# Reading relative-bias tables straight from one reversed row per head in DRAM

## The chip, the core and the metric

The kernel runs on one core of a Trainium2 chip. The core has five engines that work side by side, each through its own list of instructions in order: TensorE (PE in the profile, matrix products; its weight loads are listed as PEld), VectorE (DVE), ScalarE (ACT), GpSimd (POOL) and SyncE (SP). In this kernel every DMA is handed over by SyncE, so SyncE's list is also the order in which transfers are started; 16 DMA engines then move the data. The metric is the time of one execution on the device in microseconds (us).

## What is computed

One layer of a hybrid decoder on 512 tokens of 1024 features, in float32: a normalisation modulated by a conditioning vector, one input projection, two attention branches, a gated merge with an output projection, a squared-ReLU MLP, and a last normalisation. The change touches the additive bias of the two attention branches. Each of the 16 heads has a bias that depends on the distance between query and key alone, by a bucket of that distance:

```python
bias = rel_bias[t5_bucket(dist)][..., :SWA_Q_HEADS]            # sliding window, 8 heads
s = jnp.where(mask, s + bias, -jnp.inf)                        # window of 128 keys
...
table_b = rel_bias[:, SWA_Q_HEADS:].T                          # block attention, 8 heads
bias_own = table_b[:, t5_bucket(dist_own)]
s_own = jnp.where(dist_own >= 0, s_own + bias_own, -jnp.inf)
```

So along a diagonal of the score matrix the bias is the same: row p of a 128-row block of queries has the same list of numbers as row p + 1, moved by one key.

## The kernel before

**The list per head.** The host gives a one-hot table `onehot` of 33 rows by 1024 columns: 640 columns hold the bucket of each distance for the block attention, 384 those for the sliding window, and the 33rd row the mask. At the start of the kernel TensorE multiplies it with the bias table (L358), which gives `prv`, 16 heads by 512 columns, twice. ScalarE copies it to `rv` in SBUF (L359), and SyncE stores both halves to `rvd` in DRAM (L360): 16 rows of 1024 numbers, one row per head.

**The spread.** From there two DMAs inside DRAM make 128 copies of each row: `tsd` (L394, 8 heads x 128 x 384 numbers, for the sliding-window heads) and `tmd` (L427, 8 heads x 128 x 640 numbers, for the others). Their access pattern has the heads outermost, then the 128 copies with step 0, then the columns.

**The load per head.** `toeplitz` (L430 to L434) fills one tile of 128 partitions by 256 columns (`ts`) or 512 columns (`tm`) per head by a DMA whose row step is one number shorter than a row of the copies, so partition p reads its copy moved by p. The tiles have two buffers: a load waits until the head before the last has used its bias.

**The use.** For each head and each of its four blocks of 128 queries TensorE makes the scores (L449, `sa` or `sb`), and one VectorE instruction adds the bias and takes the row maximum (L450). A sliding-window head has blocks of 128, 256, 256 and 256 keys, a head of the block attention 128, 256, 384 and 512; a narrower block takes the last columns of the tile. ScalarE then takes the exponential (L454), TensorE transposes (L479) and multiplies with the values (L490).

**The work around it.** Every float32 product is made as three products of a high and a low part (L76 to L78); ScalarE and VectorE split each operand into the parts (L71, L72). The first stage loads the conditioning weights (`ad`, L268), makes the normalised input `hT` and the query projection of the sliding window (`g0p`). Then come the keys and values of the sliding window: `kvr` is loaded (L397), split into two pairs of weights `kvw0` and `kvw1`, and multiplied to `pkv`; `vaf` (L410) is ScalarE's copy of the values, which TensorE turns (`pva`, L416). The queries are split and their lower half is copied across partitions by a DMA (`qa`, L225), the keys likewise (`ka`, L234). The function `run` (L612) then goes through the 16 heads and between the parts of a head advances a list of dense work, in this order: values of the block attention (`proj_v`, loads `vbr`, products `pv`), its queries and keys (`proj_qk`, loads `qkr` at L550, weights `qkw`, products `pqk`), the gates (`gated`, loads `gr`), and so on. Weight loads of 1 MB (`kvr`, `vbr`, `qkr`, `gr` and the last of the `ad` tiles) share three buffers in turn (`raw`), and the split weights of 1024 columns two pairs (`wide`).

**What sets the order.** In the first stage the order on TensorE and SyncE is the written one (L331 to L391). After that a planner orders each engine's list when the program is built, from a simulated time line and the order in the code; L394 comes after the first stage, L427 inside `proj_v`. The order is fixed then, and at run time an engine waits at the first instruction of its list that isn't ready.

Of the kernel before, what the change touches and what calls it, by code (L numbers as in the profile page):

```python
# [10 lines left out]
F32 = mybir.dt.float32  # L11
F32R = mybir.dt.float32r
AF = mybir.ActivationFunctionType
ALU = mybir.AluOpType

P = 128
# [5 lines left out]
SCALE = HD ** -0.5  # L22
NH = 8
# [7 lines left out]
W_MOBA = 640  # L31
W_SWA = 384
# [5 lines left out]
def decoder_layer(ctx: ExitStack, tc: tile.TileContext, x, c, ada_w, ada_b, norm1_g, norm2_g, w_in,  # L38
# [3 lines left out]
    V, A, G, SY = nc.vector, nc.scalar, nc.gpsimd, nc.sync  # L42
# [3 lines left out]
    dr = ctx.enter_context(tc.tile_pool(name="dr", bufs=1, space=bass.MemoryType.DRAM))  # L46
# [3 lines left out]
    def bank(name):  # L50
        return ps.tile([P, 512], F32, tag="bank", name=name)

    def raw(name):
        return p0.tile([P, 2048], F32, tag="raw", name=name, bufs=3)
# [5 lines left out]
    def wide(name):  # L60
        return ptile(p0, [P, KT, P], name, "w", 2)

    def small(name):
        return ptile(p0, [P, 512], name, "s", 2)

    def scratch(name, dt=F32):
        return p0.tile([P, 512], dt, name=name, tag="t", bufs=3)

    def split(hi, lo, src):

        A.activation(hi, src, AF.Copy)  # L71
        V.tensor_tensor(lo, src, hi.bitcast(F32), op=ALU.subtract)  # L72
# [67 lines left out]
    def rows(stack):  # L140
        pst = bank("pst2")
        nc.tensor.transpose(pst[:, :64], stack, ident[:64, :64])
        V.tensor_copy(cols, pst[:, :64])
# [66 lines left out]
    with ExitStack() as sa:  # L210
# [26 lines left out]
        va = pa.tile([P, NT, 4, HD], F32R, name="va")  # L237
        sink = pz.tile([P, NH], F32, name="sink")
        rvd = dr.tile([16, W_MOBA + W_SWA], F32, name="rvd")
        tmd = dr.tile([NH, P, W_MOBA], F32, name="tmd")  # L240
        tsd = dr.tile([NH, P, W_SWA], F32, name="tsd")

        with ExitStack() as ss:
            pq = ss.enter_context(tc.tile_pool(name="pq", bufs=1))
# [110 lines left out]
            for s in range(2):  # L355
                cc = slice(s * 512, (s + 1) * 512)
                prv, rv = bank(f"prv{s}"), scratch(f"rv{s}")
                nc.tensor.matmul(prv[:16], rbx, oh[:, cc], start=True, stop=True)  # L358
                A.activation(rv[:16], prv[:16], AF.Copy)  # L359
                SY.dma_start(rvd[:, cc], rv[:16])  # L360
            rows(stack)
            next(cols_[0])
            px = bank("px0")
# [14 lines left out]
            for f in range(KT):  # L378
                for i, _ in enumerate(project(f, 2 if f == 0 else 0, NT)):
# [4 lines left out]
                    if i == 2 and f + 2 in starts:  # L384
                        n = starts[f + 2]
# [3 lines left out]
                if f + 2 < KT:  # L389
                    wgt[f + 2] = g0_split(f + 2)  # L390
            sm.close()  # L391

            wt = W_MOBA + W_SWA
            SY.dma_start(tsd, bass.AP(tensor=rvd.tensor, offset=rvd.offset + W_MOBA,  # L394
                                      ap=[[wt, NH], [0, P], [1, W_SWA]]))
            kvr = raw("kvr").rearrange("p (k n) -> p k n", k=KT)
            SY.dma_start(kvr, w0[:, :, C_KA:C_KA + 2 * P])  # L397
            pkv = []
            for s in range(2):
                w = wide(f"kvw{s}")  # L400
# [21 lines left out]
        attnT = tuple((p0.tile([P, 4, S], F32R, name=f"at{b}h", tag=f"at{b}h"),  # L422
                       p0.tile([P, 4, S], F32R, name=f"at{b}l", tag=f"at{b}l")) for b in range(2))

        def spread_moba():
            wt = W_MOBA + W_SWA
            SY.dma_start(tmd, bass.AP(tensor=rvd.tensor, offset=rvd.offset + 8 * wt,  # L427
                                      ap=[[wt, NH], [0, P], [1, W_MOBA]]))

        def toeplitz(src, h, w, n, name):  # L430
            t = pt_.tile([P, n], F32, name=f"{name}{h}", tag="tz", bufs=2)
            SY.dma_start(t, bass.AP(tensor=src.tensor, offset=src.offset + h * P * w + P - 1,
                                    ap=[[w - 1, P], [1, n]]))
            return t  # L434

        class Head:
            def __init__(self, name, q, k, g, v, dst, j, blocks, groups, widths, bias, sk):
                self.__dict__.update(locals())
                self.rows = slice(g * 64, g * 64 + 64)
                self.p = pt_.tile([P, 1280], F32, name="p" + name, tag="p", bufs=2)  # L440
                m = pz.tile([P, 4], F32, name="m" + name, tag="m", bufs=3)
                sums = pz.tile([P, 4], F32, name="u" + name, tag="u", bufs=3)
                neg = pz.tile([P, 4], F32, name="n" + name, tag="n", bufs=3)
                p, b = self.p, bias
                for i, (o, w) in enumerate(blocks):
                    e = (i + 1) * P
                    pb = bank(f"s{name}{i}")
                    for n in range(2):
                        nc.tensor.matmul(pb[:, :w], q[g][:, i * P:e], k[n][g][:, e - w:e], start=n == 0, stop=n == 1)  # L449
                    V.tensor_tensor_reduce(p[:, o:o + w], pb[:, :w], b[:, b.shape[1] - w:], scale=SCALE,  # L450
                                           scalar=-3e38 if sk is None else sk, op0=ALU.add, op1=ALU.max,
                                           accum_out=m[:, i:i + 1])
                    V.tensor_scalar(neg[:, i:i + 1], m[:, i:i + 1], -1.0, None, op0=ALU.mult)  # L453
                    A.activation(p[:, o:o + w], p[:, o:o + w], AF.Exp, bias=neg[:, i:i + 1],  # L454
                                 accum_out=sums[:, i:i + 1])
                if sk is not None:
                    es = pz.tile([P, 4], F32, name="e" + name, tag="es", bufs=2)
                    A.activation(es, neg, AF.Exp, bias=sk)
                    V.tensor_add(sums, sums, es)
                V.reciprocal(sums, sums)  # L460
                for i, (o, w) in enumerate(blocks):
                    if i == 3:
                        A.activation(p[:, o:o + w], p[:, o:o + w], AF.Copy, scale=sums[:, i:i + 1])
                    else:
                        V.tensor_scalar(p[:, o:o + w], p[:, o:o + w], sums[:, i:i + 1], None, op0=ALU.mult)
# [34 lines left out]
        def swa_head(n):  # L500
            j, g = n // 2, n % 2
            h = g * 4 + j
            return Head(f"a{h}", qa[j], ka, g, lambda kb: va[:, kb, 2 * g:2 * g + 2].rearrange("p c d -> p (c d)"), attnT[0], j,
                        [(0, 128), (128, 256), (384, 256), (640, 256)],
                        [[(0, (0, 1)), (1, (1, 2))], [(2, (2, 3)), (3, (3,))]], (256, 256, 256, 128),
                        toeplitz(tsd, h, W_SWA, 256, "ts"), sink[:, h:h + 1])

        def moba_head(n):
            i, g = n // 2, n % 2
            q, k = qk[i]  # L510
            return Head(f"b{n}", q, k, g, lambda kb: vb[:, kb, i, 2 * g:2 * g + 2].rearrange("p c d -> p (c d)"), attnT[1], i,
                        [(0, 128), (128, 256), (384, 384), (768, 512)],
                        [[(0, (0, 1, 2, 3))], [(1, (1, 2, 3)), (3, (3,))], [(2, (2, 3))]], (512, 384, 256, 128),
                        toeplitz(tmd, n, W_MOBA, 512, "tm"), None)


        def proj_v(half):
            pv = [bank(f"pv{half}{b}") for b in range(2)]
            wr = raw(f"vbr{half}").rearrange("p (k n) -> p k n", k=KT)
            SY.dma_start(wr, w0[:, :, C_VB + half * 256:C_VB + half * 256 + 256])  # L520
            if half == 0:
                spread_moba()
            for kk in range(4):
                w = tuple(v.rearrange("p (k n) -> p k n", k=2) for v in small(f"vw{half}{kk}"))
                split(w[0], w[1], wr[:, 2 * kk:2 * kk + 2])
                for k in range(2):
                    f = 2 * kk + k
                    for t in range(NT):
                        mm3(pv[t // 2][:, t % 2 * 256:t % 2 * 256 + 256], token(hT, f, t), at(w, slice(None), k),
                            first=f == 0 and t % 2 == 0, last=f == KT - 1, skip_group_check=True)  # L530
                if kk == 3:
                    for b in range(2):
                        for t in range(2):
                            i = slice(2 * half, 2 * half + 2)
                            split(vb[:, 2 * b + t, i, 0::3], vb[:, 2 * b + t, i, 1:3],
                                  pv[b][:, t * 256:t * 256 + 256].rearrange("p (i g d) -> p i g d", i=2, g=2))
                yield
# [125 lines left out]
    with ExitStack() as sb:  # L663
        pb = sb.enter_context(tc.tile_pool(name="pb", bufs=1, reuse_waits="tile"))
# [141 lines left out]
    for ci, (f0, f1) in enumerate(CHUNKS):  # L806
# [15 lines left out]
        for f in fs:  # L822
            w, ph = start(f)
# [4 lines left out]
        if not last:  # L828
            for half in range(2):
                pm = [bank(f"mo{ci}{half}{t}") for t in range(NT)]  # L830
                for f in range(f0, f1):
# [4 lines left out]
                    w = small(f"mow{ci}{half}{f}")  # L836
# [5 lines left out]
        else:  # L842
            ws = []
            for b in range(2):
                w = (p0.tile([P, 2, D], F32R, name=f"ml{b}h", tag=f"at{b}h"),
                     p0.tile([P, 2, D], F32R, name=f"ml{b}l", tag=f"at{b}l"))
                wr = raw(f"ml{b}").rearrange("p (k n) -> p k n", k=2)
                SY.dma_start(wr, wm[:, f0 + 2 * b:f0 + 2 * b + 2, :])
                for k in range(2):
                    for h in range(2):  # L850
                        cc = slice(h * 512, (h + 1) * 512)
# [6 lines left out]
            for t in range(NT):  # L858
                o = [slot(4 + 2 * (t % 2) + h, f"o{t}{h}") for h in range(2)]
                cuts = ((0, 512), (512, 1024)) if t < NT - 1 else ((0, 512), (512, 768), (768, 1024))  # L860
                sq, n = ssq[:, 4 * (t % 2):4 * (t % 2) + 4], len(cuts) - 1
# [73 lines left out]
```

## Time and profile before

| | us |
|---|---|
| three runs | 755.54, 755.74, 754.61 |
| median of the runs | 755.54 |
| the profiled execution, its own time | 753.28 |
| span of its instructions | 751.5 |
| TensorE busy | 713.4 (95%) |
| VectorE busy | 458.6 (61%) |
| ScalarE busy | 346.2 (46%) |

The profile is of one execution. Its span runs from the first to the last instruction, and the rest of the execution's own time lies around it. Rows give the line of the code (L450 is line 450), the engine, and "out <- in" by the names above. An engine's idle time is put down to what ended it ("<- DMA qkr" means that a transfer into `qkr` landed last). A busy TensorE isn't one at its peak; the clock it was granted stands beside it, 1.00 for the full one. DMA share is the mean busy share of the 16 DMA engines.

### The profile page before, as it was taken

To read this page: it belongs to the slowest core of one execution; us is meant where nothing else is said; L and a number is where in the kernel's file an instruction comes from. 1 tells how busy PE (TensorE), PEld (TensorE's weight loads), DVE (VectorE), ACT (ScalarE), POOL (GpSimd) and SP (SyncE) were. 2 spreads that over 40 slices of the span, in tenths; PEclk is the share of its full clock that TensorE was granted. 3 is DMA by queue.
4 is the path that set the end of the run, shared out by engine and by line. 5 is a ranking of instruction groups with operands and counts; after the bars stand their busy time and mean duration, and the time that the engine had idled before them with its cause. 6 is when DMAs were issued, how large, how long until landed. Compare 5 with 4: busy or idle time off the path is not lost.

```text
span 751.5 us, 9331 instructions
## 1 busy us (share of the span) xinstructions
PE 713.4 (95%) x3458; PEld 597.7 (80%) x3458; DVE 458.6 (61%) x957; ACT 346.2 (46%) x641; POOL 28.3 (4%) x40
## 2 busy tenths in 40 slices
PE   3789799999999999999999999999999999999996
PEld 1568788987788788888889888888888888888885
DVE  4862688788586975874468584253562627425765
ACT  4542687765777772343255443222342314222424
POOL 2220000000000000000030000000000000000001
PEclk9999899999899999999999999999999999999999
DMA  8986633374444575443513461333313233315103
GB/s 305 305 258 248 191 92 93 96 226 147 140 127 126 171 276 198 154 155 112 168 56 94 133 223 56 113 113 112 108 62 111 63 112 106 113 57 167 57 1 112
DMA packets 93210, 104.40 MB, mean 139 GB/s; under 512 B 3043, under 2 KB 71723, under 8 KB 93164
## 3 DMA queue, kind: packets, MB, share of 16 engines
q1 hardware_dynamic: 93164, 103.80, 44.2%
q8 instruction: 27, 0.44, 0.3%
q14 instruction: 19, 0.16, 0.1%
HBM read 98.22 MB, written 6.36 MB: 139 GB/s over the span
## 4 chain that ended last, share of the span: by engine, by line
PE 79%; DMA 8%; ACT 4%; SPq 3%; DVE 3%; issue 1%; POOLq 0%; POOL 0%; ACTq 0%; DVEq 0%
PE ph L77 8%; PE ph L78 8%; PE ph L76 8%; PE mo L78 7%; PE mo L77 7%; PE mo L76 7%; PE pg L76 3%; PE pg L78 3%; PE pg L77 3%; DMA qkr<-in_w_in_dram 2%; SPq L268 2%; DMA ad<-in_ada_w_dram 2%; PE py L78 2%; PE py L76 2%; PE py L77 2%; PE pqk L76 2%
## 5 line engine op out<-in xcount | busy, mean ns | idle before, releaser
L811 ACT ACTIVATE r<-ph 128x512 f32<-128x512 f32 x32 | 18.8, 586 | 41.2 <-PE ph L78 26.8
L814 DVE TENSOR_TENSOR r<-r 128x512 f32<-128x512 f32 x32 | 21.9, 688 | 18.2 <-ACT a2h L813 8.0
L156 DVE SCALAR_TENSOR_TENSOR ac<-a,cs,ac 128x256 f32<-128x256 f32 x56 | 26.8, 478 | 2.4 <-ACT ac L154 1.8
L296 DVE SCALAR_TENSOR_TENSOR pac<-ad,cs,pac 128x256 f32<-128x256 f32 (+1 forms) x42 | 21.4, 522 | 9.1 <-ACT pac L294 8.7
L722 DVE TENSOR_TENSOR rs<-mo,g2row 128x512 f32<-128x512 f32 x24 | 15.9, 684 | 8.8 <-PE mo L78 8.8
L186 DVE SCALAR_TENSOR_TENSOR ma<-mw,cs,ma 128x512 f32<-128x512 f32 x28 | 21.0, 749 | 0.5
L126 POOL TENSOR_TENSOR rstd<-rstd,mhalf 128x1 f32<-128x1 f32 x12 | 7.0, 587 | 375.2 <-DVE rstd L125 375.2
L454 ACT ACTIVATE pb<-pb,nb 128x128 f32<-128x128 f32 (+3 forms) x32 | 17.8, 557 | 7.2 <-DVE nb L453 6.8
L76 PE MATMUL g0p<-hTh,g0h 128*128 128x512 f32 (+1 forms) x36 | 15.1, 421 | 3.0 <-ACT hTh L71 3.0
L454 ACT ACTIVATE pa<-pa,na 128x256 f32<-128x256 f32 (+1 forms) x32 | 15.3, 478 | 3.2 <-DVE na L453 3.0
L723 DVE TENSOR_TENSOR x_sb<-x_sb,rs 128x512 f32<-128x512 f32 x24 | 16.1, 681 | 0.0
L450 DVE CUSTOM_DVE_ANT_0 pb<-sb,tm 128x128 f32<-128x128 f32 (+3 forms) x32 | 15.0, 486 | 0.2 <-PE sb L449 0.2
L450 DVE CUSTOM_DVE_ANT_0 pa<-sa,ts,sink 128x256 f32<-128x256 f32 (+1 forms) x32 | 13.6, 444 | 1.9 <-PE sa L449 1.8
L77 PE MATMUL g0p<-hTl,g0h 128*128 128x512 f32 (+1 forms) x36 | 14.1, 392 | 0.1
L78 PE MATMUL g0p<-hTh,g0l 128*128 128x512 f32 (+1 forms) x36 | 13.8, 384 | 0.0
L449 PE MATMUL sb<-qk,qk 128*128 128x128 f32 (+3 forms) x64 | 12.9, 331 | 0.0
L449 PE MATMUL sa<-ka,qa 128*128 128x256 f32 (+1 forms) x64 | 11.7, 297 | 0.0
L301 PEld LDWEIGHTS pac<-ones_r,acc 128*128 128x128 f32 x32 | 5.0, 224 | 8.3 <-DVE acc L296 5.7
L284 POOL TENSOR_TENSOR g0l<-g0r,g0h 128x512 fp32r<-128x512 f32 x8 | 10.3, 1293 | 27.6 <-ACT g0h L283 27.6
L301 PE MATMUL pac<-ones_r,acc 128*128 128x1 f32 x32 | 5.3, 274 | 6.1 <-DVE acc L296 6.1
L852 DVE TENSOR_TENSOR ml<-ml,g2row 128x512 f32<-128x512 f32 x8 | 5.1, 687 | 9.9 <-DMA ml<-in_w_mlp_out_dram 9.9
L723 POOL TENSOR_TENSOR x_sb<-x_sb,rs 128x512 f32<-128x512 f32 x4 | 5.0, 1290 | 157.0 <-DVE rs L722 157.0
(1599 smaller groups left out, 2431.7 us busy)
## 6 DMA issues: line engine op xcount, KB each, us to landing
mi<-in_w_mlp_in_dram SPq DMA_DIRECT2D x16, 1024.0 KB, 5.6
mo<-in_w_mlp_out_dram SPq DMA_DIRECT2D x14, 1024.0 KB, 5.1
ad<-in_ada_w_dram SPq DMA_DIRECT2D x16, 512.0 KB, 7.3
a<-in_ada_w_dram SPq DMA_DIRECT2D x16, 512.0 KB, 5.2
gr<-in_w_in_dram SPq DMA_DIRECT2D x8, 1024.0 KB, 6.3
mw<-in_ada_w_dram SPq DMA_DIRECT2D x8, 1024.0 KB, 5.2
x_sb<-in_x_dram SPq DMA_DIRECT2D x8, 512.0 KB, 6.6
qkr<-in_w_in_dram SPq DMA_DIRECT2D x4, 1024.0 KB
```

The lines of the kernel that those rows point to most:

```text
L76: nc.tensor.matmul(o, w[0], m[0], start=first, stop=False, **kw)
L77: nc.tensor.matmul(o, w[0], m[1], start=False, stop=False, **kw)
L78: nc.tensor.matmul(o, w[1], m[0], start=False, stop=last, **kw)
L156: V.scalar_tensor_tensor(acc, ad[:, k], cs[:, k:k + 1], acc, op0=ALU.mult, op1=ALU.add)
L186: V.scalar_tensor_tensor(acc, t[:, k], c1, acc, op0=ALU.mult, op1=ALU.add)
L296: V.scalar_tensor_tensor(part_ if k < KT - 1 else acc, ad(k), cs[:, k:k + 1], part_, op0=ALU.mult, op1=ALU.add)
L449: nc.tensor.matmul(pb[:, :w], q[g][:, i * P:e], k[n][g][:, e - w:e], start=n == 0, stop=n == 1)
L450: V.tensor_tensor_reduce(p[:, o:o + w], pb[:, :w], b[:, b.shape[1] - w:], scale=SCALE, scalar=-3e38 if sk is None else sk, op0=ALU.add, op ...
L454: A.activation(p[:, o:o + w], p[:, o:o + w], AF.Exp, bias=neg[:, i:i + 1], accum_out=sums[:, i:i + 1])
L723: add.tensor_tensor(x_sb[:, t, cc], x_sb[:, t, cc], tm, op=ALU.add)
L811: A.activation(r, ph, AF.Relu)
L814: V.tensor_mul(r, r, r)
```

## The change

The copies `tsd` and `tmd` and the DMAs that fill them are gone. `rv` is now made by VectorE, and with its columns in reverse; the two halves are stored in each other's place, so each row of `rvd` as a whole runs backward. The load of a head reads 128 rows straight from the one row of that head, each beginning one number after the row before, so the rows overlap. With the list reversed this step forward has the effect of the old step backward; the columns of the tile then stand in reverse, and the VectorE instruction reads its bias operand backward.

```diff
-        tmd = dr.tile([NH, P, W_MOBA], F32, name="tmd")
-        tsd = dr.tile([NH, P, W_SWA], F32, name="tsd")
...
-                A.activation(rv[:16], prv[:16], AF.Copy)
-                SY.dma_start(rvd[:, cc], rv[:16])
+                V.tensor_copy(rv[:16], prv[:16, ::-1])
+                SY.dma_start(rvd[:, 512 - s * 512:1024 - s * 512], rv[:16])
...
-            wt = W_MOBA + W_SWA
-            SY.dma_start(tsd, bass.AP(tensor=rvd.tensor, offset=rvd.offset + W_MOBA,
-                                      ap=[[wt, NH], [0, P], [1, W_SWA]]))
...
-        def spread_moba():
-            wt = W_MOBA + W_SWA
-            SY.dma_start(tmd, bass.AP(tensor=rvd.tensor, offset=rvd.offset + 8 * wt,
-                                      ap=[[wt, NH], [0, P], [1, W_MOBA]]))
-
-        def toeplitz(src, h, w, n, name):
+        def toeplitz(h, c0, n, name):
+
             t = pt_.tile([P, n], F32, name=f"{name}{h}", tag="tz", bufs=2)
-            SY.dma_start(t, bass.AP(tensor=src.tensor, offset=src.offset + h * P * w + P - 1,
-                                    ap=[[w - 1, P], [1, n]]))
+            SY.dma_start(t, bass.AP(tensor=rvd.tensor, offset=rvd.offset + h * (W_MOBA + W_SWA) + c0,
+                                    ap=[[1, P], [1, n]]))
             return t
...
-                    V.tensor_tensor_reduce(p[:, o:o + w], pb[:, :w], b[:, b.shape[1] - w:], scale=SCALE,
+                    V.tensor_tensor_reduce(p[:, o:o + w], pb[:, :w], b[:, w - 1::-1] if w < b.shape[1] else b[:, ::-1], scale=SCALE,
                                            scalar=-3e38 if sk is None else sk, op0=ALU.add, op1=ALU.max,
...
-                        toeplitz(tsd, h, W_SWA, 256, "ts"), sink[:, h:h + 1])
+                        toeplitz(h, 1, 256, "ts"), sink[:, h:h + 1])
...
-                        toeplitz(tmd, n, W_MOBA, 512, "tm"), None)
+                        toeplitz(NH + n, 1 + W_SWA, 512, "tm"), None)
...
-            if half == 0:
-                spread_moba()
```

## The prediction

> **What bounds the kernel now.** I read the page first, then the waits of TensorE, the chain, and the timelines around the place they name.
>
> ```profile
> PE 713.4 (95%) x3458; PEld 597.7 (80%) x3458; DVE 458.6 (61%) x957; ACT 346.2 (46%) x641; POOL 28.3 (4%) x40
> PE pva L416 <- ACT vaf L410: 5.0, 1, 5.0
> PE pkv L76 <- ACT kvw0h L71: 2.7, 1, 2.7
> ```
>
> TensorE is busy 95% of the span, so only its few gaps can pay. The last two lines are the longest of its waits between 35 and 110 us: 5.0 us for the tile vaf and, earlier, 2.7 us for kvw0h. The chain says what ended last before the longer one:
>
> ```profile
> 44.30 10.09 DMA vbr<-in_w_in_dram
> ...
> 64.76 17.15 DMA qkr<-in_w_in_dram
> 82.00 1.06 ACT qkw01h L71
> 83.08 0.61 ACT vaf L410
> 83.73 1.12 PE pva L416 x4
> ```
>
> vaf needs nothing from qkr. It stands behind qkw01h in ScalarE's order, and qkw01h waits for a 1 MB weight load that the chain dates 17.15 us back. The timelines of SyncE, ScalarE, TensorE and VectorE (start, duration, what, wait before):
>
> ```profile
> 44.30 0.52 SPq L520 DMA_DIRECT2D vbr<-in_w_in_dram  x1
> 44.92 3.11 SPq L394 DMA_DIRECT2D tsd<-rvd  x1
> 48.13 6.49 SPq L427 DMA_DIRECT2D tmd<-rvd  x1
> 54.71 16.29 SPq L550 DMA_DIRECT2D qkr<-in_w_in_dram  x2
> 71.09 3.47 SPq L225 DMA_DIRECT2D qa<-qa0l  x1
> 77.82 1.06 ACT L71 ACTIVATE qkw00h<-qkr 128x1024 fp32r<-128x1024 f32 x1 [7.14 <-DMA qkr<-in_w_in_dram]
> 69.66 0.39 PE L78 MATMUL pkv<-hTh,kvw0l 128*128 128x512 f32 x1
> 74.65 0.39 PE L78 MATMUL pkv<-hTh,kvw1l 128*128 128x512 f32 x1
> 78.47 0.28 PE L78 MATMUL pv<-vw01h,hTl 128*128 128x256 f32 x1
> 83.73 1.12 PE L416 MATMUL pva<-ident,vaf 128*128 128x128 f32 x4 [4.98 <-ACT vaf L410]
> 45.48 0.47 DVE L296 SCALAR_TENSOR_TENSOR acc<-ad,cs,pac 128x256 f32<-128x256 f32 x1
> 58.52 1.21 DVE L72 TENSOR_TENSOR kvw1l<-kvr,kvw1h 128x1024 fp32r<-128x1024 f32 x1
> ```
>
> Between vbr and qkr stand the two spread copies, tsd and tmd. SyncE hands vbr over in 0.52 us but is held 3.11 and 6.49 us by the spreads, and 16.29 us by the two qkr loads behind them. I read this as a queue that is full, so that everything later (qa0l at 71.09) waits too. What the queue does in that time is in the table by stretches (length, busy us of PE, PEld, DVE, ACT, POOL, granted clock, DMA share, GB/s; the sum is that of six stretches from 85 to 280); the last line is from the list of DMA issues, with KB and us to landing:
>
> ```profile
> 54.00:65.00 11.00, 8.04 (x36) 6.66 (x35) 4.56 (x5) 4.79 (x7) 1.35 (x1) 0.84 0.53 204
> 57.00:62.00 5.00, 4.70 (x21) 4.17 (x22) 3.27 (x3) 2.21 (x4) 0.51 (x1) 0.66 0.53 205
> 79.00:84.00 5.00, 0.27 (x2) 0.27 (x2) 3.43 (x4) 2.45 (x4) 0.00 (x0) 0.85 0.46 125
> 84.00:89.00 5.00, 5.00 (x24) 4.86 (x24) 4.88 (x14) 4.82 (x8) 0.00 (x0) 0.50 0.32 67
> 85.00:145.00 60.00, 60.00 (x397) 55.18 (x396) 48.66 (x168) 46.89 (x121) 1.63 (x3) 0.96 0.40 113
> 240.00:260.00 20.00, 18.41 (x96) 15.38 (x95) 17.81 (x49) 17.97 (x36) 0.00 (x0) 1.00 0.46 132
> sum 195.00, PE 189.60 PEld 164.32 DVE 153.36 ACT 144.57 POOL 4.23; mean PE 31.60 PEld 27.39 DVE 25.56 ACT 24.09 POOL 0.71
> gr<-in_w_in_dram SPq DMA_DIRECT2D x8, 1024.0 KB, 6.3
> ```
>
> For 11 us half of the DMA engines move 204 GB/s and the rest stand idle. By the shapes in the code the spreads write 8 x 128 x (384 + 640) numbers of 4 bytes, 4.19 MB, which at 204 GB/s is 20.6 us. The stretch from 84 to 89 shows a second price: after the 5 us gap TensorE runs at 0.50 of its clock.
>
> *The skill on this.* The Trainium skill (DMA: Bandwidth & Descriptors, Rules for kernel authors) says that a DMA whose outermost dimension is under 16 is confined to that many engines; here it is 8 heads, and the share of 0.53 agrees with that. Spread over all engines at twice the rate, 4.19 MB would take 10 us, both qkr loads would be there before 78.5, and taking the spreads away would save nothing; the row of 204 GB/s is what gives the change its worth.
>
> **The change, part by part.**
>
> *The two spreads go* (L394, L427). qkr's first load then follows vbr on SyncE. Its buffer, the third of the raw ones, was last read by the sum acc that ended at 45.95, so it can be issued at about 46; behind vbr, which landed at 54.4 (44.30 + 10.09), it lands by 54.4 + 6.3 (the 1 MB row) = 60.7 at the latest. The second load takes kvr's buffer, free when kvw1l ends at 59.73, and lands by 66.0. ScalarE's splits of them then wait for weight buffers only (two in the pair): qkw00h from 70.05 (last matmul on kvw0l), qkw01h from 75.04 (on kvw1l), so vaf ends at 75.04 + 1.06 + 0.61 = 76.7, before TensorE has done pv at 78.75. The copies of qa and ka that the first scores need, held behind qkr on SyncE until 71.09, go out as soon as their splits end. So the 4.98 us go. What is late next is TensorE's own work. With the gap goes the half clock: 0.27 us before 84, 5.00 us up to 89 at 0.50, and a little after: 5.3 / 2 = 2.7 us. **Sum of this part: 4.98 + 2.7 = 7.7 us.** From 85 to 145 TensorE is busy without a break, and the later loads are issued as buffers come free, so I let all later work move with it.
>
> *The first gap (2.7 us) stays.* It ends with vbr, queued ahead of the spreads, so their packets come behind it. By 0, at the least; bounded above by the whole gap and its half clock (rival A).
>
> *The copy of the rows moves from ScalarE to VectorE, reversed* (L359), and each half is stored in the other's place; two issues as before.
>
> ```profile
> 4.32 3.57 PE L358 MATMUL prv<-oh,rbx 33*16 33x512 f32 x4 [1.58 <-DMA oh<-in_onehot_dram]
> 9.03 1.05 ACT L359 ACTIVATE rv<-prv 16x512 f32<-16x512 f32 x2
> 9.13 3.13 DVE L296 SCALAR_TENSOR_TENSOR pac<-ad,cs,pac 128x512 f32<-128x512 f32 x4 [5.97 <-ACT pac L294]
> 31.71 8.46 DMA ad<-in_ada_w_dram
> ```
>
> VectorE stands idle 5.97 us, and prv is complete at 7.9 in it, so at least the first copy and most of the second fit in. A backward read from PSUM isn't in the trace: between 0.5 us each (ScalarE's) and twice that. Were they put behind the first sums instead, VectorE would be 1 to 2 us late at 9 to 13; what covers that is the stream of ad loads, which the chain follows up to 40.17 (31.71 + 8.46), and without it the 1 to 2 us would count. I take 0.
>
> *The bias loads read overlapping rows.* Their count, shape and issue stay; 128 pieces of 1 or 2 KB now come from 1.5 to 2.6 KB of DRAM.
>
> ```profile
> tm<-tmd SPq DMA_DIRECT2D x8, 256.0 KB, 2.7
> g1row<-in_ada_b_dram SPq DMA_DIRECT2D x2, 256.0 KB, 5.9
> 97.58 0.33 SPq L432 DMA_DIRECT2D ts<-tsd  x1
> 105.31 0.32 SPq L432 DMA_DIRECT2D ts<-tsd  x1
> ```
>
> Reading one row 128 times is in the trace: g1row, a row of 2 KB sent to all partitions, takes 5.9 us, tm now 2.7. Two buffers give a load about one head's time, 105.31 − 97.58 = 7.7 us. So 0; a load would have to take over 7.7 us, beyond the upper row, to be late. The first load now waits on SyncE for the store of rvd, as tsd did at 44.92, and for its memory, which the first stage had; what is queued behind it then is rival B.
>
> *VectorE reads the bias backward* (L450), 64 times.
>
> ```profile
> L450 DVE CUSTOM_DVE_ANT_0 pb<-sb,tm 128x512 f32<-128x512 f32 x8 | 5.5, 684 | 0.0
> L450 DVE CUSTOM_DVE_ANT_0 pb<-sb,tm 128x384 f32<-128x384 f32 x8 | 4.4, 549 | 0.2 <-PE sb L449 0.2
> ```
>
> A column costs (684 − 549) / 128 = 1.05 ns, one element after the other; nothing in that speaks for a price on direction. Lower bound 0. Upper: every column twice, 8 x 896 + 8 x 1280 = 17,408 columns (the blocks of the heads in the code), 18.3 us of VectorE. It is busy 81% from 85 to 145, so that hides there, but at 240 to 260 (17.81 of 20) some 2 us would show. I take 0, nearest to the forward rows.
>
> **Sum:** 753.3 (the profiled execution's own time, span 751.5) − 7.7 = 745.6. The median of the runs is 755.5, 2.2 above that execution; on their scale I forecast 755.5 − 7.7 = **747.8**, own range 745 to 750.
>
> **The rivals.**
>
> *A. The early gap goes as well.* A new planned order may let ScalarE split kvr before vbr; DRAM writes also no longer run beside the loads. Against: vbr's packets were queued before the spreads. Price: 2.7 us, and the loss of clock behind it, (1 − 0.66) x 5 us in 57 to 62, 1.7 us. Time 747.8 − 4.4 = 743.4.
>
> *B. A wait on SyncE takes the spreads' place.* In the order of the code the first bias load comes before the qkr loads. Planned so, it holds SyncE until its memory is free, at the latest when the first stage's last product is done (second row below: g0p).
>
> ```profile
> 84.50 1.63 PE L449 MATMUL sa<-ka,qa 128*128 128x128 f32 x6
> 67.85 0.39 PE L78 MATMUL g0p<-hTh,g0l 128*128 128x512 f32 x1
> ```
>
> That is 68.24, and qkr's first load lands at 68.24 + 6.3 = 74.5. Now the first scores start 84.50 − 77.82 = 6.7 us after qkw00h; from 74.5 that makes 81.2, a gap of 2.5 us after 78.75, with half clock behind it, 1.7 us as after the first gap. Of the 7.7 us 4.2 are given back: 755.5 − 3.5 = 752.0. For it: the code's order; against: the planner already put qkr ahead. By the Trainium skill (TensorE: Matmul & The Clock Gate, What's actually happening) the clock drops after an idle window of about 3.4 us; by that, the gap alone would count, 750.3. The trace differs: 2.7 us of idling before 57 were followed by a mean of 0.66 in 57 to 62.
>
> *C. Nothing gained:* the 5 us turn up again at a later wait (VectorE has 2.2 us left in 240 to 260). For it speaks that a delay shared by all engines can let one of them catch up; against, that TensorE had no break from 85 to 145. 755.5.
>
> *D. Slower: the backward read costs several times a forward one.* It would decide once VectorE has no room in the heads' stretch, 85 to 280, where it is busy 153.4 of 195 us: 41.6 us, plus the 7.7 gained, at 18.3 us per further column time, so from 3.7 times on. At four times: 54.9 − 41.6 − 7.7 = 5.6 us lost, 761. Against: the 1.05 ns.
>
> **How the numbers follow.** Forecast 0.52, A 0.15, B 0.13, C 0.11, D and other ways to lose 0.09. Range: A less the runs' spread of 1.1 us (754.61 to 755.74) gives 742.3, B plus it 753.1; outside lie C and D, 0.20. A measurement of this kernel tells about 0.2%, 1.5 us, from no change: forecast, A and B are faster (0.80), C the same (0.11), D slower (0.09).
>
> **What would show it.** In the changed profile: no DMA at half share after vbr; 4.19 MB less written to HBM; each qkr issue under 1 us unless a buffer isn't free; no 5 us wait of pva for vaf, and no clock of 0.50 after it; L450 still at 684 ns for 512 columns; tm landing in 3 to 6 us. The forecast is wrong if TensorE still has a gap of some us between the last pv of the first half and the first scores, or if its waits after 145 grow by what was saved.

## The result and the profile after

| | before | after |
|---|---|---|
| median of four runs (us) | 755.08 | 746.21 |
| lowest and highest (us) | 751.73, 755.74 | 745.23, 747.35 |
| the profiled execution, its own time (us) | 753.28 | 745.23 |
| span (us) | 751.5 | 743.5 |

The ratio is 0.9892, with a 95% interval from 0.9859 to 0.9925. The unchanged pair was timed twice more on other chips, beside the experiments below: 0.9921 (0.9899 to 0.9943) and 0.9935 (0.9908 to 0.9962). The three medians lie 8.9, 6.3 and 5.9 us below those of before; by the ratios it is 8.2, 6.0 and 4.9. The forecast was 7.7, and the intervals of the two repeats end at 7.6 and 6.9 us, a little short of it. Four executions in the groups of this document took 1029 to 4053 us; the medians count them, the ratios do not.

The page of the changed kernel; after it stand its waits of TensorE between 35 and 110 us (what TensorE waited for: us in total, times, longest):

```profile
PE 709.7 (95%) x3458; PEld 595.6 (80%) x3458; DVE 459.1 (62%) x959; ACT 344.6 (46%) x639; POOL 28.7 (4%) x40
HBM read 94.03 MB, written 2.16 MB: 129 GB/s over the span
```

The same line of the page of before:

```profile
HBM read 98.22 MB, written 6.36 MB: 139 GB/s over the span
```

And the waits:

```profile
PE pac L299 <- DVE acc L294: 1.5, 1, 1.5
PE ta L470 <- DVE pa L456: 1.2, 1, 1.2
PE pkv L76 <- ACT kvw0h L71: 1.0, 1, 1.0
PE pkv L76 <- ACT kvw1h L71: 0.2, 1, 0.2
```

Of the 6.36 MB written before, 4.20 MB are gone: the two spread copies. Of the waits, the 5.0 us of `pva` for `vaf` is gone altogether. The wait for `kvw0h` is still there, shorter in this execution. A new one has come, 1.2 us of the first transposes (`ta`) for VectorE.

The timelines of SyncE and ScalarE around the place (start, duration, what, idle time before with its releaser):

```profile
44.36 0.57 SPq L511 DMA_DIRECT2D vbr<-in_w_in_dram  x1
47.24 12.48 SPq L539 DMA_DIRECT2D qkr<-in_w_in_dram  x2
65.31 0.52 SPq L225 DMA_DIRECT2D qa<-qa0l  x1
65.92 1.02 SPq L423 DMA_DIRECT2D ts<-rvd  x2
```

```profile
67.83 1.06 ACT L71 ACTIVATE qkw00h<-qkr 128x1024 fp32r<-128x1024 f32 x1 [1.31 <-PE pkv L77]
72.82 1.06 ACT L71 ACTIVATE qkw01h<-qkr 128x1024 fp32r<-128x1024 f32 x1 [1.33 <-PE pkv L77]
73.90 0.60 ACT L405 ACTIVATE vaf<-pkv 128x512 f32<-128x512 f32 x1
```

`qkr` now goes out at 47.24 where before it was 54.71. The 12.48 us are its second load, which waits for the buffer of `kvr`; nothing else is held. The splits of `qkr` are released by TensorE ("<-PE pkv"), that is by weight buffers coming free, and no longer by the DMA. So `vaf` ends at 73.90 + 0.60 = 74.50, and TensorE reaches its transposes later than that. First the tile's row of after, then that of before (count, ns of one as min/median/max, from first start to last):

```profile
L411 PE MATMUL pva<-ident,vaf x4: 272/272/273, 76.7 to 77.0; 128*128 128x128 f32 x4
```

```profile
L416 PE MATMUL pva<-ident,vaf x4: 421/421/477, 83.7 to 84.4; 128*128 128x128 f32 x4
```

The same four transposes start 7.0 us earlier, and take 272 ns where they took 421, because no half clock follows a gap any more. The stretches of after (length, busy us of PE, PEld, DVE, ACT, POOL, granted clock, DMA share, GB/s):

```profile
54.00:65.00 11.00, 9.74 (x50) 7.73 (x49) 4.96 (x6) 5.39 (x8) 1.34 (x1) 1.00 0.45 141
57.00:62.00 5.00, 4.79 (x29) 3.94 (x28) 2.93 (x3) 1.81 (x3) 0.11 (x1) 1.00 0.23 57
74.00:84.00 10.00, 10.00 (x86) 10.00 (x85) 9.46 (x30) 8.21 (x18) 0.52 (x1) 1.00 0.51 134
84.00:89.00 5.00, 3.76 (x22) 3.02 (x21) 3.96 (x14) 4.98 (x19) 0.00 (x0) 1.00 0.64 157
```

From 74 to 84 TensorE is busy without a break at full clock; that is the stretch in which it stood still for 5 us. Between 57 and 62 the DMA engines have little to do, because both `qkr` loads are either done or still waiting for their buffer.

How the 8.0 us between the two spans come about: 7.0 us are there when `pva` starts. About 2.7 us are added by the half clock that before showed from 84 to 89 (5.3 us busy at 0.50, counted as in the prediction) and after shows no more. The new wait of `ta` takes 1.2 us back. That is 8.5, and the rest of the span changes little: from 250 us to the end TensorE's products start 8.1 us earlier than before (median over the products of each stretch of 10 us).

The 7.0 us are more than the wait of 4.98 because TensorE was 2.0 us ahead before it came to that wait: the early gap for `kvw0h` was smaller in this execution, 1.0 us, with no loss of clock behind it. This early gap is not the same in every execution, as the experiments show, so it is not put down to the change.

### The profile page after: what moved, and what is told of

The parts are those of the page before. It is cut to its first block, busy times and chain, and to the rows that moved or that the text cites. A ratio compares the mean times of both kernels' runs of the same rounds, so it can differ in the third digit from the quotient of the medians.

```text
span 743.5 us, 9326 instructions
## 1 busy us (share of the span) xinstructions
PE 709.7 (95%) x3458; PEld 595.6 (80%) x3458; DVE 459.1 (62%) x959; ACT 344.6 (46%) x639; POOL 28.7 (4%) x40
## 4 chain that ended last, share of the span: by engine, by line
PE 84%; ACT 4%; DMA 4%; DVE 3%; SPq 2%; issue 1%; POOL 0%; POOLq 0%; ACTq 0%; DVEq 0%
PE ph L77 8%; PE ph L76 8%; PE ph L78 8%; PE mo L78 7%; PE mo L76 7%; PE mo L77 7%; PE pg L76 3%; PE pg L78 3%; PE pg L77 3%; PE pqk L76 2%; PE py L78 2%; PE pqk L77 2%; PE py L76 2%; PE pqk L78 2%; PE py L77 2%
## 5 line engine op out<-in xcount | busy, mean ns | idle before, releaser
L76 PEld LDWEIGHTS g0p<-hTh,g0h 128*128 128x128 f32 x36 | 8.0, 222 | 5.1 <-ACT hTh L71 4.5
L470 PE MATMUL tb<-ident,pb 128*128 128x128 f32 x80 | 10.6, 274 | 0.3 <-DVE mb L441 0.3
```

What stands on the lines that cost most here:

```text
L76: nc.tensor.matmul(o, w[0], m[0], start=first, stop=False, **kw)
```

## The experiments

Each median stands beside runs of the kernel before on the same chip. Runs with spreads "read by nobody" do extra work whose result is not used.

**The theory** is the prediction's: the spreads run on half of the DMA engines, hold SyncE and delay the `qkr` loads, and TensorE waits for these. **Its rivals:** the bytes cost time wherever they are moved; the planner's new order brought the gain; the new form of the loads or of the copy brought or cost something.

### The spreads kept, but on all engines

The 128 copies become the outermost dimension. Bytes, destinations and the order of every engine stay as before.

```diff
-            SY.dma_start(tsd, bass.AP(tensor=rvd.tensor, offset=rvd.offset + W_MOBA,
-                                      ap=[[wt, NH], [0, P], [1, W_SWA]]))
+            SY.dma_start(tsd.rearrange("h p w -> p h w"), bass.AP(tensor=rvd.tensor, offset=rvd.offset + W_MOBA,
+                                                                  ap=[[0, P], [wt, NH], [1, W_SWA]]))
...
-            SY.dma_start(tmd, bass.AP(tensor=rvd.tensor, offset=rvd.offset + 8 * wt,
-                                      ap=[[wt, NH], [0, P], [1, W_MOBA]]))
+            SY.dma_start(tmd.rearrange("h p w -> p h w"), bass.AP(tensor=rvd.tensor, offset=rvd.offset + 8 * wt,
+                                                                  ap=[[0, P], [wt, NH], [1, W_MOBA]]))
```

> The kernel before with one thing changed: the two spreads write the same 4.19 MB with the 128 copies outermost instead of the 8 heads. The order of every engine's list is that of before. Queue theory (the spreads hold the queue because they run on half of the DMA engines): DMA share near 1 after vbr, the spreads done by about 64 us, both qkr loads landed by about 72, no 5 us wait of TensorE for vaf and no half clock after it; 755.1 - 7.7 = 747.4, between 746 and 749. Planner theory (the gain came from the new order of the lists): 755, since the order is the old one. Traffic theory (the gain is that of 4.19 MB less to move): 755, since the bytes are the same.

Measured: 749.67 beside 753.78, ratio 0.9946 (0.9923 to 0.9968). Its waits, its timelines of SyncE and ScalarE, its stretches, and its list of DMA issues (KB, us from issue to landing):

```profile
PE pva L416 <- ACT vaf L410: 2.6, 1, 2.6
```

```profile
47.23 3.29 SPq L427 DMA_DIRECT2D tmd<-rvd  x1
50.61 12.42 SPq L550 DMA_DIRECT2D qkr<-in_w_in_dram  x2
...
77.05 1.06 ACT L71 ACTIVATE qkw01h<-qkr 128x1024 fp32r<-128x1024 f32 x1 [2.67 <-DMA qkr<-in_w_in_dram]
78.13 0.60 ACT L410 ACTIVATE vaf<-pkv 128x512 f32<-128x512 f32 x1
```

```profile
54.00:57.00 3.00, 1.33 (x6) 0.48 (x4) 2.29 (x3) 3.00 (x5) 1.34 (x1) 1.00 1.07 146
57.00:62.00 5.00, 5.00 (x30) 4.50 (x31) 2.27 (x3) 1.15 (x2) 0.00 (x0) 1.00 1.00 338
```

```profile
tmd<-rvd SPq DMA_DIRECT2D x1, 2560.0 KB, 22.5
```

What follows: with the order of all instructions and all the bytes unchanged, 4.1 us are gained. The changed kernel gained 6.3 in the same comparison (753.78 to 747.52), so some two thirds of the gain hang on the engines the spreads ran on (the two intervals overlap; the wait that is left, 2.6 us, is what tells the two apart). Neither the planner nor the bytes can have brought that part. The 749.67 lies outside the 746 to 749 that the queue theory gave: it had the second `qkr` load there by 72, and `qkw01h` waited for it until 77.05.

The other third is left, and the trace shows that the spreads did not take half the time on twice the engines. All engines are busy (1.07 and 1.00), but in one stretch they move only 146 GB/s. The large spread landed at 47.23 + 22.5 = 69.7, `qkw01h` still waits for a DMA, and `vaf` ends at 78.7, 4 us later than in the changed kernel.

The rule that the prediction cited (the Trainium skill, DMA: Bandwidth & Descriptors, Rules for kernel authors: an outermost dimension under 16 confines the DMA to that many engines) agrees with the share, 0.53 before and 1.00 here. What the prediction worked out from it, that on all engines the spreads would cost nothing, does not hold.

### The spreads with the heads as 4 x 2

The heads were to be split into two dimensions, 4 and 2, so that only four engines would be used.

```diff
-            SY.dma_start(tsd, bass.AP(tensor=rvd.tensor, offset=rvd.offset + W_MOBA,
-                                      ap=[[wt, NH], [0, P], [1, W_SWA]]))
+            SY.dma_start(tsd.rearrange("(a b) p w -> a b p w", b=2), bass.AP(tensor=rvd.tensor, offset=rvd.offset + W_MOBA,
+                                      ap=[[2 * wt, 4], [wt, 2], [0, P], [1, W_SWA]]))
...
-            SY.dma_start(tmd, bass.AP(tensor=rvd.tensor, offset=rvd.offset + 8 * wt,
-                                      ap=[[wt, NH], [0, P], [1, W_MOBA]]))
+            SY.dma_start(tmd.rearrange("(a b) p w -> a b p w", b=2), bass.AP(tensor=rvd.tensor, offset=rvd.offset + 8 * wt,
+                                      ap=[[2 * wt, 4], [wt, 2], [0, P], [1, W_MOBA]]))
```

> The kernel before with the heads of the two spreads written as 4 times 2, so that the outermost dimension is 4; bytes and the order of every list as before. Queue theory: 4 engines, half the rate, about 102 GB/s and a DMA share of 0.27; the spreads end some 21 us later, so qkr and vaf come about 20 us later and the gap of 5 us becomes about 25: about 775, between 770 and 780. Planner and traffic theory: 755.

Measured: one time, 754.51 beside 753.78. Its stretch and its wait:

```profile
54.00:65.00 11.00, 10.68 (x54) 8.54 (x53) 5.14 (x6) 4.74 (x8) 1.36 (x1) 1.00 0.53 199
```

```profile
PE pva L416 <- ACT vaf L410: 7.4, 1, 7.4
```

The edit did not lower the number of engines: the share is 0.53 again. The two dimensions lie behind one another without a hole, so they may have been taken as one of 8; the run doesn't show it. Either way it doesn't test the theory. It serves as a second profile of the kernel before, though. In it the early gap for `kvw0h` is absent (clock 1.00), and yet `pva` starts at 83.4, as late as with a gap of 2.7 us (83.7), since the wait for `vaf` has grown to 7.4. Before the change the landing of `qkr` set the end of this stage, and what TensorE lost ahead of it cost nothing.

### Both spreads put back, read by nobody

The changed kernel, with both copies in their old places.

```diff
+        tmd = dr.tile([NH, P, W_MOBA], F32, name="tmd")
+        tsd = dr.tile([NH, P, W_SWA], F32, name="tsd")
...
+            wt = W_MOBA + W_SWA
+            SY.dma_start(tsd, bass.AP(tensor=rvd.tensor, offset=rvd.offset,
+                                      ap=[[wt, NH], [0, P], [1, W_SWA]]))
...
+        def spread_moba():
+            wt = W_MOBA + W_SWA
+            SY.dma_start(tmd, bass.AP(tensor=rvd.tensor, offset=rvd.offset + 8 * wt + W_SWA,
+                                      ap=[[wt, NH], [0, P], [1, W_MOBA]]))
...
+            if half == 0:
+                spread_moba()
```

> The changed kernel with the two spreads put back in their places on 8 engines, but read by nobody; the bias is still loaded from the single rows and read backward. Queue theory: SyncE is held by qkr until about 71 again, the wait for vaf is back: 753 to 756. Theory that the direct reading itself gives the gain: 746. Planner theory: near 746 if the planned order is that of the changed kernel, which it is not quite (it is planned anew).

Measured: 754.10 beside 753.78, ratio 1.0018 (0.9997 to 1.0038). Its wait and its SyncE:

```profile
PE pva L416 <- ACT vaf L410: 6.1, 1, 6.1
```

```profile
54.24 16.29 SPq L551 DMA_DIRECT2D qkr<-in_w_in_dram  x2
```

The wait is back, the `qkr` issues are held 16.29 us as before, and the whole gain is gone. All the rest of the change (overlapping rows, backward reading, the copy on VectorE) is in this kernel, and together it is worth less than the measurement can tell. (What it does ahead of the wait for `vaf` could hide in that wait; the two runs with the copy on ScalarE and with one buffer, below, bear on that.) The planner's new order is in it too: in the traces TensorE's 3458 products stand in the same order as in the changed kernel, and the lists of ScalarE and VectorE differ from its lists in the place of one instruction each. With the spreads back, that order gains nothing.

### One spread put back, read by nobody

The small one (8 x 128 x 384 numbers, 1.57 MB) alone, and the large one (8 x 128 x 640, 2.62 MB) alone, with the same lines as above.

> The changed kernel with only the small spread (1.57 MB, sliding-window heads) put back on 8 engines, read by nobody. At 200 GB/s it holds its engines 7.8 us, from about 51.5 to 59.5. Queue theory with a threshold: what counts is whether the second qkr load lands before ScalarE could use it, at about 75; it lands near 66, so there is no wait for vaf and the time is that of the changed kernel, about 747. Theory of a price per byte: three eighths of the whole loss of 6 to 9 us, 749 to 751.

> The changed kernel with only the large spread (2.62 MB, block-attention heads) put back on 8 engines, read by nobody: 13 us of the queue, to about 64.5. Queue theory with a threshold: the second qkr load lands near 71, still before 75, so about 747 again, at most 1 us more. Price per byte: five eighths, 750.5 to 752.

Measured: 746.45 with the small spread, ratio 0.9891 (0.9857 to 0.9924); 747.16 with the large one, ratio 0.9904 (0.9867 to 0.9941); the kernel before had 755.17 beside them. The changed kernel itself was not timed on this chip; the nearest to it there is the version with the copy on ScalarE below, 746.38. Neither run has a wait for `vaf`, and `pva` starts at 77.4 and 79.6:

```profile
L416 PE MATMUL pva<-ident,vaf x4: 272/272/273, 77.4 to 77.8; 128*128 128x128 f32 x4
L413 PE MATMUL pva<-ident,vaf x4: 270/272/272, 79.6 to 80.0; 128*128 128x128 f32 x4
```

So the gain is not proportional to the bytes taken away: taking away either of the two gives all of it that can be measured. It is a matter of a margin: `qkr` only has to land before TensorE is through with its own work. With the large spread alone SyncE began to hand over the first `qkr` load at 48.99, much as in the changed kernel (47.24), and the load still landed only 19.3 us after that, where it took 9.6 there; so it is also late by what stands ahead of it in the queue, and not only by its place in SyncE's list.

### The large spread moved to a later place

The kernel before, with its bytes and its 8 engines, but the large spread is issued after the second `vbr` load; a copy of 64 bytes makes it wait for that load.

```diff
-            if half == 0:
+            if half == 1:
+                SY.dma_start(tmd[0, 0:1, 0:16], wr[0:1, 0, 0:16])
                 spread_moba()
```

> The kernel before, bytes and 8 engines kept, but the large spread made to wait for the second vbr load (by a 64-byte store of that load into its target first), so that it goes out after the qkr loads, at about 90. Queue theory: the wait for vaf is gone as in the changed kernel; instead the spread runs beside the next loads from 90 to 103, where the queue has little to do (share 0.10 from 95 to 100 before): 747 to 750. Traffic theory: no gain, 754.

Measured: 746.10 beside 755.17, ratio 0.9899 (0.9869 to 0.9928). Its SyncE, and the stretch behind it:

```profile
88.17 0.71 SPq L427 DMA_DIRECT2D tmd<-rvd  x1
```

```profile
90.00:103.00 13.00, 13.00 (x78) 11.41 (x78) 10.13 (x36) 11.02 (x28) 0.58 (x1) 1.00 0.71 246
```

All 4.19 MB are still copied, one of the copies among the heads, where TensorE stays busy 13.00 of 13 us at full clock while the DMA engines move 246 GB/s. The time is that of the changed kernel. The rival that the bytes cost time wherever they move is refuted: what cost was that both copies stood ahead of `qkr` (the small one still does here). The line of SyncE also bears out that the queue was full before: the same issue that held SyncE for 6.49 us there takes 0.71 us here.

### The reversed copy on ScalarE

```diff
-                V.tensor_copy(rv[:16], prv[:16, ::-1])
+                A.activation(rv[:16], prv[:16, ::-1], AF.Copy)
```

> The changed kernel with the reversed copy of the rows on ScalarE instead of VectorE. In the changed kernel's profile the two copies (0.67 us each) stood among the first sums of VectorE, at 11.65 and 12.91, and the first stage ran 1.1 us later than before. If the copies cost that, this kernel is 1 us faster than the changed one (746); if the ad loads merely landed later, or the later stage hides it, it is the same within 1 us (747).

Measured: 746.38 beside 755.17, ratio 0.9892 (0.9853 to 0.9931). The engine that makes the copy can't be told in the time. But the run changes two things, for with this edit the planner goes back to the order of before: TensorE's 3458 products stand as in the kernel before, not as in the changed kernel, and the lists of ScalarE and VectorE differ from those of before in the place of one instruction each.

That settles the rival of the planner. The old order without the spreads takes 746.38, the new order with both spreads 754.10 (on another chip, where the kernel before took 753.78). The gain goes with the spreads and not with the order.

### One buffer for the bias

```diff
-            t = pt_.tile([P, n], F32, name=f"{name}{h}", tag="tz", bufs=2)
+            t = pt_.tile([P, n], F32, name=f"{name}{h}", tag="tz", bufs=1)
```

> The changed kernel with one buffer instead of two for the bias tiles, so that no load of a head is covered by the head before. Landing is 3.1 to 7.1 us per load in the changed kernel. If the second buffer is what hides the overlapping-row loads, each of the 16 heads' scores come some 3 us later; as dense products fill TensorE between, part of 16 x 3 = 48 us shows: 750 to 780. If dense work hides it anyway: 747.

Measured: one time, 749.04 beside 752.15. Its waits of VectorE, its waits of TensorE, and its stretch:

```profile
DMA ts<-rvd: 1.4, 2
```

```profile
PE pkv L76 <- ACT kvw0h L71: 3.3, 1, 3.3
```

```profile
57.00:62.00 5.00, 3.76 (x13) 3.12 (x14) 3.78 (x4) 3.37 (x5) 1.34 (x1) 0.50 0.02 6
```

Even without a second buffer VectorE waits only 1.4 us in all for the overlapping loads, and the longest wait of TensorE for VectorE behind that is 2.3 us. Most of what this run took above the changed kernel goes with an early gap of 3.3 us and half clock behind it. One execution can't give the price of the second buffer more closely; that two buffers leave room to spare, as the prediction had it, is what the trace of the changed kernel shows, where VectorE never waits for a bias load.

### The first projection-weight load of the third part held back

In the changed kernel the early gap ends with `vbr`, which shares the DMA engines with other loads. Here the first load of `w_branch_a` (`br`) has to wait until the gate before it (`before`) is made, so that `vbr` is alone.

```diff
                     br = p0.tile([P, 4, 256], F32, name=f"br{s}{m}", tag="br")
+                    if s == 0 and m == 0:
+                        V.tensor_copy(br[:, 0, 0:1], before[:, 0:1])
```

> The changed kernel with one thing more: the first load of w_branch_a (0.5 MB, not used before about 140), which SyncE hands over just ahead of kvr and vbr, is made to wait for the first gate, by a one-column VectorE copy into its tile. With the spreads gone the early gap before pkv counts by itself: 1.05 us in the changed kernel's profile, 2.75 with 1.7 of clock in that of before. Queue theory: kvr and vbr come 1.4 us (two issues) to 2.5 us earlier, the gap shrinks or goes: 1 to 3 us under the changed kernel, 744 to 746. Rival: the planner's new list lets ScalarE wait for vbr ahead of the split of hT, which gives it back: 747 or more.

Measured: 747.17 beside 752.15, ratio 0.9925 (0.9906 to 0.9944). The unchanged new kernel beside it:

> The changed kernel again, beside the one above on the same chip, and for one more profile: 746 to 748; the early gap between 0 and 2.8 us, no wait for vaf, first transpose pva between 76 and 80.

It had 746.26, ratio 0.9935 (0.9908 to 0.9962). With the load held back the early gap is gone and `pva` starts at 75.8, but a wait has come later:

```profile
PE py L76 <- ACT bw00h L71: 2.1, 1, 2.1
```

The weight that was held back is late in its turn: its load went out at 182.23 only, behind the gate. The 744 to 746 that were expected did not come. This is no better version; the two can't be told apart. In the profile of the unchanged new kernel on this chip the early gap was 0.3 us without any edit.

### The new kernel on the chip of the first experiments

> The changed kernel once more, for a second profile and a narrower interval: 746, between 745 and 747.5. If the small first gap (1.05 us instead of 2.75) and the full clock after it belong to the change, they are there again; if they came from ad loads that happened to land 1.1 us late in that execution, the gap is near 2.7 us again, with half clock behind it, and this execution is 1 to 2 us longer.

Measured: 747.52 beside 753.78, ratio 0.9921 (0.9899 to 0.9943). It gave no profile that can be read beside the others, so the question about the first gap is answered by the run on the other chip alone: 0.3 us there, at full clock.

## Why the prediction was right, point by point

**The 4.98 us of `vaf`: right in cause.** The wait is gone in every run that took one or both spreads out from ahead of `qkr`, and comes back (6.1 us) when both do. That it is what stands ahead in the queue, and not the bytes as such, the late spread shows. The amount is the length of the wait in one execution: in the second profile of before it was 7.4 us, at the same end.

**The chain behind it: right in kind.** The two `qkr` loads landed at 56.8 (47.24 + 9.6) and 65.0 us, where the prediction had 60.7 at the latest and 66.0. It had `vaf` end at 76.7, set by weight buffers; it ended at 74.50, set by weight buffers. It was earlier because TensorE was 2.0 us ahead by then in that execution. "What is late next is TensorE's own work" held.

**The half clock, 2.7 us: right.** 84 to 89 went from 0.50 to 1.00. The new wait of `ta` for VectorE, 1.2 us, was not in the sum. It comes with the planner's new order: the version with both spreads put back has that order and has the wait too, though its `pva` starts at 82.8; the late spread and the copy on ScalarE have the order of before and no such wait, with `pva` at 78.4 and 77.1.

**The sum, 7.7 us: near, and in part by luck.** The spans of the two profiles differ by 8.0 us. The sum lacked the 2.0 us that TensorE was ahead before the wait and the 1.2 us of `ta`; they have opposite signs and partly cancel. By the two repeats the gain is smaller, 6.0 and 4.9 us.

**The first gap "stays", price 0: right, though the reasoning lacked a half.** It varies with no change to the kernel, and no tie to the spreads can be seen: 2.7 and 0 us in the two profiles of before, 0.3 and 1.0 in two of after, 3.3 with one buffer. What the prediction missed is that it changed its worth. Before the change the landing of `qkr` covered it (83.7 with it, 83.4 without); after the change TensorE's own work sets the end, and the gap counts. So the gain is not one number for all executions. The one-buffer version's `pva` started at 80.3, after 3.3 us of early gap. The changed kernel's started at 76.7 in one profile and at 77.7 in another, where this gap was the smaller one, 0.3 us, but TensorE's waits for `acc` came to 3.5 us instead of 1.5. So it is all that TensorE loses ahead of this place that counts now.

**The copy, price 0: the price was right, the place wrong.** The prediction put both copies into VectorE's idle time before its first sums. They came among the sums (VectorE's timeline after):

```profile
10.20 1.55 DVE L294 SCALAR_TENSOR_TENSOR pac<-ad,cs,pac 128x512 f32<-128x512 f32 x2 [7.05 <-ACT pac L292]
11.65 0.67 DVE L357 COPY rv<-prv 16x512 f32<-16x512 f32 x1
12.25 0.73 DVE L294 SCALAR_TENSOR_TENSOR pac<-ad,cs,pac 128x512 f32<-128x512 f32 x1
12.91 0.67 DVE L357 COPY rv<-prv 16x512 f32<-16x512 f32 x1
```

They take 0.67 us each, inside the bounds of 0.5 and 1.0. The cover named for that case, the stream of `ad` loads, was enough as far as the times show: with the copies on ScalarE (and the order of before) the time is the same.

**The overlapping rows, price 0: right.** The new kernel's landing times (us, min/median/max), for the tiles `tm` and then `ts`:

```profile
DMA to landing us min/median/max: 3.2/3.5/7.1
DMA to landing us min/median/max: 3.1/3.3/5.1
```

`tm` took 2.7 before, so a load from overlapping rows takes some 0.8 us more by the medians, within the 3 to 6 us that were named. The longest, 7.1 us, lies above them and only just below the 7.7 us of cover; no wait of VectorE for a bias load shows in the trace.

**The backward read, price 0: right.** VectorE's groups after, by shape:

```profile
L441 DVE CUSTOM_DVE_ANT_0 pb<-sb,tm 128x512 f32<-128x512 f32 x8 | 5.5, 686 | 0.0
L441 DVE CUSTOM_DVE_ANT_0 pb<-sb,tm 128x384 f32<-128x384 f32 x8 | 4.4, 552 | 0.2 <-PE sb L440 0.2
```

686 and 552 ns where forward it was 684 and 549. Rival D is out.

**The other rivals.** A (the early gap goes as well) is not shown: the gap was smaller in the new kernel's profiles, but one profile of before had none. B (SyncE held by the first bias load) did not come: the planner put the load at 65.92, behind `qkr`. C (the 5 us turn up again later) did not either; TensorE is busy from 74 to 84, and its products still start 8.1 us earlier at the end.

**What the cited rule was made to say: wrong.** "Taking the spreads away would save nothing" if they ran on all engines: they were put on all engines, and taking them away is still worth about 2 us by the medians (749.67 to 747.52; the intervals overlap), and the trace still has 2.6 us of the wait. The step that failed is the one that doubled the rate with the engines.

## What to carry to other kernels

A DMA that nobody is waiting for yet can still set the end, when it stands ahead of an urgent load in the same queue: look for issues that take microseconds instead of half of one, and at the DMA share in that time. Here a share near one half, with an engine waiting behind it, went with copies that run on part of the engines; moving one behind the urgent load, putting them on all engines or taking them out each helped, and the first is an edit of two lines. A gain of this kind ends where the waiting engine's own work begins, so it is the difference between two ends and not the length of the wait, and half the cut may bring all of it.

## What was not expected of the hardware

- **All engines were not twice as fast as half of them.** The spreads on 16 engines showed a share of 1.07 at 146 GB/s from 54 to 57, and 1.00 at 338 GB/s from 57 to 62; on 8 engines 0.53 at 204. In the first of these stretches each engine moved less than before. Whether it is the writing from all engines into one region of memory, or the loads beside it, was not tried.
- **Splitting the outermost dimension did not lower the number of engines.** 4 x 2 heads that lie behind one another gave the same share as 8 (0.53).
- **A short gap can cost the clock.** After waits for `kvw0h` of 1.0 and 1.5 us the clock from 57 to 62 was 1.00; after 1.8 us it was 0.66 (the version with the small spread, lines below), after 2.7 us 0.66, after 3.3 us 0.50. These are means over 5 us: stretch by stretch the clock in the traces read here is either 1.00 or 0.50, and it stays at 0.50 for 3.4 us (57.15 to 60.56 with the small spread, 58.63 to 62.05 in the kernel before) or for twice or three times that (82.53 to 89.35 in the kernel before, around the end of the 5 us gap). The skill's figure (the Trainium skill, TensorE: Matmul & The Clock Gate, What's actually happening) is an idle window of about 3.4 us. Here a gap of half that was followed by a lower clock; how the hardware counts the window, these profiles don't show.

```profile
PE pkv L76 <- ACT kvw0h L71: 1.8, 1, 1.8
...
57.00:62.00 5.00, 5.00 (x23) 4.63 (x24) 2.17 (x3) 1.07 (x2) 0.00 (x0) 0.66 0.77 199
```

- **Direction is free for VectorE here.** A two-operand float32 instruction that reads one operand backward took 686 ns for 512 columns where forward it took 684.
